# Hybrid encoder block on one core: output tiles between the attention's last blocks, first loads of the second layer on GpSimd's queue, results added one a step

## The chip, the cores and the metric

The kernel runs on one NeuronCore of a Trainium2 chip. Five engines work side by side: TensorE (PE, with its weight loads shown as PEld), VectorE (DVE), ScalarE (ACT), GpSimd (POOL) and SyncE (SP), which issues DMAs. Each engine takes its own instructions in order and waits on semaphores for the others. The metric is the device time of one execution in microseconds, as the median of several runs; lower is better.

## The reference

One block of a streaming encoder on 1024 tokens (and 16 meta tokens in front, dropped at the end) of width 1024, all in float32:

```
u = rmsnorm(h, norm_mix);  z = u @ w_in            # pool input, q, k, v, r, low rank gate, ga, gb
y_a = pooled means (windows 2, 4, 8, 16) mixed by group, scaled, @ w_pool_out
y_b = (rmsnorm(chunked gated linear attention(q, k, v)) * silu(r)) @ w_gla_out
h = h + (sigmoid(ga) * y_a + sigmoid(gb) * y_b) @ w_out
u = rmsnorm(h, norm_ffn)
h = h + square(relu(u @ w_ff1)) @ w_ff2            # 1024 -> 4096 -> 1024
out = rmsnorm(h, norm_final)
```

## The kernel before

**Products.** Every float32 operand of a product is split in two: ACT makes a rounded high part (`act.activation(hi, a, ACT.Copy)`), DVE or GpSimd subtracts it to get the low part, and `mm3` (L250) issues three matmuls of 128x512 for each pair of operand tiles. So each loaded weight costs a DMA, an ACT operation and a DVE operation before PE can use it.

**Order.** PE's instructions run in the order in which the program writes them (L1463). The order of the other engines, SP's queue of DMA issues included, is made by a planner from its own model of the times, with the program's order as priority; on the chip each of these engines then works its list in order and waits at whatever is not ready.

**From the attention to the first layer.** Tokens are two halves of 512. The list `one` holds the steps. `gla` (L1099) runs the attention and fills PE's gaps with other blocks, last the four `yb_block(j, 0)` of the first half. What follows is the second half: `yb_block(j, 1)` (L859), j = 0 to 3, each 24 matmuls on a quarter of w_gla_out, merged by DVE with the gates (`t<-gb_dram`) and the pooled part (`o<-ma_dram`), L880 to L885, into `MH`, `ML`. `out_tile(t, 0)` (L1182) multiplies 128 tokens of the merged result with the first 512 columns of w_out, 24 matmuls, and adds x, which lies in `acc` (L1195). Tiles 0 to 3 read the first half only, 4 to 7 the second. Its weights `wo` come in four quarters, `load_wo(0, k)` (L1157): quarter k holds contraction tiles 2k and 2k + 1, in the order in which the tile uses them. `x_again` (L1153) loads x into `acc`, eight tiles.

**Raw buffers.** Both kinds of weights land in raw buffers that `Raw.load` (L93) takes in rotation; there are two, and a third is lent by `merge_open` (L1150). The ring `W1` (L57) holds the split form of two blocks: `top_up` (L66) loads the block after the next one as soon as a block has issued its last matmul ("free", L879), and it issues load and split in one go, so a raw buffer stays taken until the ring's slot is free and both split operations are done. In the program, the load of block j + 2 stands at the end of block j.

**Second layer.** The first layer writes seven combinations of its squared results to DRAM (`keep`, L1304), from SP's queue. The second layer, `ff2` (L1401), is a Strassen-like scheme of seven products, m = 0 to 6, of 16 steps each. A step multiplies one loaded tile `a` (`ff2_load`, L1346, into one of four half buffers) with one weight tile (`ff2_weight`, L1351; the four quarters of w_ff2 stay in SBUF) or a sum of two (`bt`, L1375), for four token tiles t: 12 matmuls. Operands are split two steps ahead into seven slots. The accumulators are four PSUM banks of eight, in turn. After a product's last step the program adds all its results to `c` (`leave`, L1411): one or two DVE operations a token tile, for m = 4 also the finished rows of tokens 512 to 1023 (`finish_row`, L1379), for m = 5 the last normalization's upper half (L1435 to L1439), for m = 6 the other rows, which end the program.

Of the kernel before, what the change touches and what calls it, by code (L numbers as in the profile page):

```python
# [10 lines left out]
ACT = mybir.ActivationFunctionType  # L11
ALU = mybir.AluOpType
AX = mybir.AxisListType

P = 128
# [4 lines left out]
HALF = 512  # L20
# [83 lines left out]
def kernel(  # L104
# [3 lines left out]
    nc = tc.nc  # L108
    x = x[0]
# [50 lines left out]
    gB = left.push("gB", [P, D], F32)  # L160
# [27 lines left out]
    def f32(ap):  # L188
        return ap.bitcast(F32)
# [4 lines left out]
    def bcast(v):  # L194
        return v[None, :].broadcast_to([P, D])
# [248 lines left out]
    def halves():  # L444
        return [slice(h * HALF, (h + 1) * HALF) for h in range(2)]
# [213 lines left out]
    one = []  # L659
# [122 lines left out]
    def rows4(w, j):  # L782
        return w[:, j * 256 : (j + 1) * 256].rearrange("(k p) c -> p k c", p=P)
# [75 lines left out]
    def yb_block(j, h):  # L859
        def fn(wb):  # L860
            hi, lo = (t.rearrange("p (k c) -> p k c", k=4) for t in wb)
            assert h or ("o", 0) in done
            yg = S["yg"][h]
            for e in range(2):
                d, w = 2 * j + e, slice(e * P, (e + 1) * P)
                yb_load(d, h)
                yb_load(d + 1, h)
                if S["dt1"] > 3:
                    yb_load(d + 2, h)
                gl, ml = staged[d, h]  # L870
                b = bank("mm")
                for k in range(4):
                    mm3(
                        b, 1, lambda i: (hi[:, k, w], lo[:, k, w]),
                        lambda i: (yg[:, 0, k], yg[:, 1, k]), first=k == 0, last=k == 3,
                    )
                    yield 3 * 512 / 2400
                if e:
                    yield "free"  # L879
                dve.tensor_tensor(gl, b, gl, ALU.mult)  # L880
                dve.tensor_tensor(gl, gl, ml, ALU.add)
                th = MH[h][:, d]
                tl = ML[h][:, d]
                act.activation(th, gl, ACT.Copy)
                pool.tensor_tensor(tl, gl, f32(th), ALU.subtract)  # L885

        return fn
# [250 lines left out]
    def merge_open():  # L1138
        W1.eng = dve
        banks(keep=2, ms=3)  # L1140
        left.pop_to(base)
        right.pop_to(1)
        S["wo"] = [left.push("wo0", [P, 2, KT, HALF], F32R)]
        S["left_acc"] = left.mark()
        S["acc"] = left.push("acc", [P, 8, D], F32)
        buffer("u2", 2, D)
        S["left2"] = left.mark()
        buffer("t1", 4)
        buffer("o", 4)
        raw.lend(left.push("raw3", [P, D], F32))  # L1150
        nc.sync.dma_start(gB, bcast(norm_ffn))

    def x_again():  # L1153
        for t in range(8):
            nc.sync.dma_start(S["acc"][:, t], x[t * P : (t + 1) * P, :])

    def load_wo(ch, kk):  # L1157
        def fn():
            wo = S["wo"][ch][:, :, 2 * kk : 2 * kk + 2]
            c = slice(ch * HALF, (ch + 1) * HALF)  # L1160
            r = raw.load(w_out[kk * 256 : (kk + 1) * 256, c].rearrange("(k p) c -> p k c", p=P), D)
            r = r.rearrange("p (k c) -> p k c", k=2)
            act.activation(wo[:, 0], r, ACT.Copy)
            dve.tensor_tensor(wo[:, 1], r, f32(wo[:, 0]), ALU.subtract)

        return fn
# [15 lines left out]
    def out_tile(t, ch):  # L1182
        def fn():
            half, at = t // 4, (t % 4) * P
            wo = S["wo"][ch]
            b, n = bank("mm"), ORDER.index(t)
            for j in range(2):
                if ch and j and n > 1:
                    turn_tile(ORDER[n - 2])
                mm3(  # L1190
                    b, KT // 2, lambda i: (MH[half][:, 4 * j + i, at : at + P], ML[half][:, 4 * j + i, at : at + P]),
                    lambda i: (wo[:, 0, 4 * j + i], wo[:, 1, 4 * j + i]), first=j == 0, last=j == 1,
                )
# [38 lines left out]
            dve.tensor_tensor(fl, a, f32(fh), ALU.subtract)  # L1232

    yb = lambda j: step(one, yb_block(j, 1), W1, [rows4(w_gla_out, j)])
    yb(0)
    for k in range(4):
        step(one, load_wo(0, k))
    yb(1)
    yb(2)
    step(one, x_again)  # L1240
    step(one, out_tile(0, 0))
    yb(3)
    step(one, out_tile(1, 0))
    step(one, wo1_open)
    for t in range(2, 8):
        step(one, out_tile(t, 0))
        if t < 6:
            step(one, load_wo(1, t - 2))

# [52 lines left out]
    hf_of = {m: hf_dram[n] for n, (m, _, _) in enumerate(FF2)}  # L1302
# [42 lines left out]

    def ff2_load(m, i):  # L1346
        at = S["a2"][(m * NPAIR + i) % len(S["a2"])]
        nc.sync.dma_start(at, hf_of[FF2[m][0]][i])
        return at

    def ff2_weight(q, i):  # L1351
        j, k = int(q[0]) - 1, int(q[1]) - 1
        f = 2 * i + j
        nc.sync.dma_start(S["w2"][q][:, i], w_ff2[f * P : (f + 1) * P, k * HALF : (k + 1) * HALF])

    def ff2_raw():
        for m in range(7):
# [21 lines left out]
    def finish_row(t, tail):  # L1379

        a, (h0, h1) = S["c"][:, t], halves()
        junk = S["w2"]["12"].rearrange("p i c -> p (i c)")[:, (t % 4) * D : (t % 4 + 1) * D]
        if not tail:
            ss = ln_stat[t % 4]
            act.activation(junk, a, ACT.Square, accum_out=ss)
            rs = inv_sqrt(ss, 1, 1.0 / D)
            dve.scalar_tensor_tensor(junk, a, rs, gB, ALU.mult, ALU.mult)
# [12 lines left out]

    def ff2():  # L1401
        nc.sync.dma_start(gB, bcast(norm_final))
        h1 = halves()[1]
        b, late = None, []

        def product(t, i, av, bv):
            (ah, al), (bh, bl) = av, bv
            c = slice(t * P, (t + 1) * P)
            mm3(b[t], 1, lambda _: (ah[:, c], al[:, c]), lambda _: (bh, bl), first=i == 0, last=i == NPAIR - 1)

        def leave(m, t):  # L1411
            for r, k, sign in FF2[m][2]:
                a = S["c"][:, 4 * r + t, k * HALF : (k + 1) * HALF]
                if sign > 0:
                    dve.tensor_tensor(a, b[t], a, ALU.add)
                else:
                    dve.tensor_tensor(a, a, b[t], ALU.subtract)

        for m, i, av, bv in ahead(ff2_operands(), 2):
            if i == 0:  # L1420
                b = [bank("o") for _ in range(4)]
            if m == 6 and i >= NPAIR - 3:
                late.append((i, av, bv))
            else:
                for t in range(4):
                    product(t, i, av, bv)
            if i < NPAIR - 1:
                continue
            for t in range(4):
                for x in late:  # L1430
                    product(t, *x)
                leave(m, t)
                if m == 4:
                    finish_row(4 + t, False)
                elif m == 5:  # L1435
                    a = S["c"][:, t, h1]
                    junk = S["w2"]["12"][:, 8 + t]
                    act.activation(junk, a, ACT.Square, accum_out=tails[t][1])
                    dve.tensor_tensor(a, a, gB[:, h1], ALU.mult)  # L1439
                elif m == 6:  # L1440
                    finish_row(t, True)

    def ff_layers():

# [59 lines left out]
```

## Time and profile before

| | |
|---|---|
| median of 3 runs | 1255.62 us (1255.46 to 1256.19) |
| the profiled execution | 1256.39 us |
| its span, first to last instruction | 1254.6 us |
| granted clock of TensorE, mean | 0.998 |
| busy: PE, DVE, ACT, POOL | 97%, 68%, 50%, 5% |
| DMA | 175.40 MB, 140 GB/s over the span |

Busy times are sums over stages with different limits, so the profile is read stage by stage: which engine waits, for how long, and what ended the wait. A row of the timeline gives start, duration, engine, source line and operation, and in brackets the idle time ahead of it with what ended it. SPq rows are DMA issues.

### The profile page before, as it was taken

The numbers are of one execution on the slowest core, as the hardware profiler recorded it, in microseconds if no ns is written. First come the engines' busy times: TensorE is split into PE (matmuls) and PEld (weight loads), VectorE is DVE, ScalarE is ACT, GpSimd is POOL, SyncE is SP. The second block draws the span as 40 slices with busy tenths as digits, with TensorE's granted clock in tenths as the row PEclk, the third lists the DMA queues.
The fourth block names the chain that finished last, engine by engine and source line by source line (L and its number), as shares of the span: only waits on it lengthen the run. The fifth ranks groups of instructions, "written<-read, shape, count | busy, mean of one in ns | idle before, by whom it ended". The sixth has DMA issues, their size and how long they took to land.

```text
span 1254.6 us, 18159 instructions
## 1 busy us (share of the span) xinstructions
PE 1212.4 (97%) x6799; PEld 1001.8 (80%) x6799; DVE 850.0 (68%) x1404; ACT 625.4 (50%) x1101; POOL 57.5 (5%) x37
## 2 busy tenths in 40 slices
PE   3999999999999999999999999999999999999997
PEld 2888888988897877788878888888878788888776
DVE  6776667564355766842897776766764877887686
ACT  7557747431345565422664554554553444445544
POOL 0000000001000114500000000000000000000000
PEclk9999999999999999999999999999999999999999
DMA  8023334417211236850244544544569863333532
GB/s 265 1 67 109 110 92 127 142 54 249 85 36 35 86 109 194 302 202 37 81 130 150 167 150 143 168 145 149 164 221 380 271 231 108 96 98 88 173 89 88
DMA packets 143863, 175.40 MB, mean 140 GB/s; under 512 B 11008, under 2 KB 83472, under 8 KB 143776
## 3 DMA queue, kind: packets, MB, share of 16 engines
q1 hardware_dynamic: 143776, 174.25, 43.4%
q8 instruction: 53, 0.87, 0.3%
q14 instruction: 34, 0.28, 0.1%
HBM read 120.74 MB, written 53.48 MB: 139 GB/s over the span
## 4 chain that ended last, share of the span: by engine, by line
PE 90%; DVE 4%; ACT 2%; DMA 2%; issue 2%; SPq 0%; DVEq 0%; ACTq 0%
PE b_mm L254 9%; PE b_mm L256 9%; PE b_mm L255 9%; PE b_o L255 8%; PE b_o L256 8%; PE b_o L254 8%; PE b_y L254 5%; PE b_y L255 5%; PE b_y L256 5%; PE b_z L254 3%; PE b_z L255 3%; PE b_z L256 3%; PE b_sc L255 3%; PE b_sc L254 3%; PE b_sc L256 3%
## 5 line engine op out<-in xcount | busy, mean ns | idle before, releaser
L254 PE MATMUL b_mm<-th,w1h 128*128 128x512 f32 (+1 forms) x240 | 86.1, 359 | 0.0
L255 PE MATMUL b_mm<-tl,w1h 128*128 128x512 f32 (+1 forms) x240 | 83.9, 349 | 0.0
L256 PE MATMUL b_mm<-th,w1l 128*128 128x512 f32 (+1 forms) x240 | 83.7, 349 | 0.0
L272 ACT ACTIVATE w1h<-raw 128x512 fp32r<-128x512 f32 x96 | 59.6, 623 | 43.3 <-PE b_sc L255 14.1
L254 PE MATMUL b_sc<-th,w1h 128*128 128x512 f32 x192 | 76.8, 400 | 2.0 <-ACT u2p L364 2.0
L254 PE MATMUL b_o<-w1h 128*128 128x512 f32 x192 | 75.0, 390 | 2.8 <-DVE h L1312 1.8
L255 PE MATMUL b_sc<-tl,w1h 128*128 128x512 f32 x192 | 76.3, 398 | 0.3 <-DVE tl L199 0.3
L255 PE MATMUL b_o<-w1l,w1h 128*128 128x512 f32 x192 | 75.0, 390 | 1.4 <-DVE w1l L273 1.4
L256 PE MATMUL b_sc<-th,w1l 128*128 128x512 f32 x192 | 75.8, 395 | 0.0
L256 PE MATMUL b_o<-w1h,w1l 128*128 128x512 f32 x192 | 74.8, 390 | 0.1
L273 DVE TENSOR_TENSOR w1l<-raw,w1h 128x512 fp32r<-128x512 f32 x96 | 65.6, 684 | 10.9 <-ACT w1h L272 10.9
L272 ACT ACTIVATE w1h<-fs 128x512 fp32r<-128x512 f32 x72 | 45.4, 631 | 49.9 <-PE b_y L255 34.4
L254 PE MATMUL b_z<-th,w1h 128*128 128x512 f32 x160 | 62.5, 391 | 0.4 <-DVE c L618 0.4
L255 PE MATMUL b_z<-tl,w1h 128*128 128x512 f32 x160 | 62.4, 390 | 0.4 <-DVE tl L1224 0.4
L256 PE MATMUL b_z<-th,w1l 128*128 128x512 f32 x160 | 62.3, 389 | 0.0
L273 DVE TENSOR_TENSOR w1l<-fs,w1h 128x512 fp32r<-128x512 f32 x72 | 49.3, 685 | 17.9 <-ACT w1h L272 17.9
L1375 DVE TENSOR_TENSOR bt<-w,w 128x512 f32<-128x512 f32 x80 | 54.6, 683 | 1.7 <-DMA w<-in_w_ff_dram 1.7
L272 ACT ACTIVATE w1h<-bt 128x512 fp32r<-128x512 f32 x44 | 27.6, 629 | 54.6 <-issue 31.4
L254 PEld LDWEIGHTS b_mm<-th,w1h 128*128 128x128 f32 x240 | 45.0, 188 | 8.8 <-issue 2.3
L254 PE MATMUL b_mm<-wo,th 128*128 128x512 f32 x128 | 50.4, 394 | 0.0
L256 PEld LDWEIGHTS b_mm<-th,w1l 128*128 128x128 f32 x240 | 45.1, 188 | 6.0
L256 PE MATMUL b_o<-fxh,fxl 128*128 128x512 f32 x128 | 49.9, 390 | 0.0
(334 smaller groups left out, 3386.7 us busy)
## 6 DMA issues: line engine op xcount, KB each, us to landing
hf_dram<-h SPq DMA_DIRECT2D x112, 256.0 KB, 2.1
raw<-hf_dram SPq DMA_DIRECT2D x112, 256.0 KB, 2.7
w<-in_w_ff_dram SPq DMA_DIRECT2D x64, 256.0 KB, 4.9
raw<-in_w_in_dram SPq DMA_DIRECT2D x24, 512.0 KB, 4.7
raw<-in_w_ff_dram SPq DMA_DIRECT2D x16, 512.0 KB, 4.2
rawx<-in_w_ff_dram SPq DMA_DIRECT2D x16, 512.0 KB, 4.1
xs<-in_x_dram SPq DMA_DIRECT2D x8, 512.0 KB, 5.6
rawx<-in_w_in_dram SPq DMA_DIRECT2D x8, 512.0 KB, 4.5
```

What stands on the lines that cost most here:

```text
L254: pe.matmul(ps, ah, bh, start=first and i == 0, stop=False, skip_group_check=more)
L255: pe.matmul(ps, ah, bl, start=False, stop=False, skip_group_check=more)
L256: pe.matmul(ps, al, bh, start=False, stop=last and i == n - 1, skip_group_check=more)
L272: act.activation(hi, a, ACT.Copy)
L273: dve.tensor_tensor(lo, a, f32(hi), ALU.subtract)
L1375: dve.tensor_tensor(bt, w, S["w2"][q[3:]][:, i], ALU.add if q[2] == "+" else ALU.subtract)
```

## The change

Three parts. The order of steps at the end of the attention: out tiles 0 and 1 of the first half stand after the second and third of the last blocks instead of after the third and fourth, three of the four quarters of w_out are loaded after the second block, and each out tile loads its own x tile. The load of norm_ffn's weights into `gB` moves from `merge_open` to the out tile 4. In the second layer, the loads of steps 0 to 3 of the first product, hf tiles and weight quarter "11", eight DMAs, go through GpSimd's queue. The results of products 0 to 5 are kept in a list `owed`, and each later step issues one entry; those of the last product are issued at once as before.

```
-        nc.sync.dma_start(gB, bcast(norm_ffn))
-    def x_again():
-        for t in range(8):
-            nc.sync.dma_start(S["acc"][:, t], x[t * P : (t + 1) * P, :])
+    def x_again(t):
+        nc.sync.dma_start(S["acc"][:, t], x[t * P : (t + 1) * P, :])
...
+    def out_(t):
+        def fn():
+            x_again(t)
+            if t == 4:
+                nc.sync.dma_start(gB, bcast(norm_ffn))
+            out_tile(t, 0)()
+        step(one, fn)
     yb(0)
-    for k in range(4):
+    step(one, load_wo(0, 0))
+    yb(1)
+    for k in range(1, 4):
         step(one, load_wo(0, k))
-    yb(1)
+    out_(0)
     yb(2)
-    step(one, x_again)
-    step(one, out_tile(0, 0))
+    out_(1)
     yb(3)
-    step(one, out_tile(1, 0))
     step(one, wo1_open)
     for t in range(2, 8):
-        step(one, out_tile(t, 0))
+        out_(t)
         if t < 6:
             step(one, load_wo(1, t - 2))
...
     def ff2_load(m, i):
-        nc.sync.dma_start(at, hf_of[FF2[m][0]][i])
+        queue(m, i).dma_start(at, hf_of[FF2[m][0]][i])
+    def queue(m, i):
+        return pool if m == 0 and i < 4 else nc.sync
     def ff2_weight(q, i):
-        nc.sync.dma_start(S["w2"][q][:, i], ...)
+        (queue(0, i) if q == "11" else nc.sync).dma_start(S["w2"][q][:, i], ...)
...
+        def add(b, t, r, k, sign):
+            a = S["c"][:, 4 * r + t, k * HALF : (k + 1) * HALF]
+            if sign > 0:
+                dve.tensor_tensor(a, b, a, ALU.add)
+            else:
+                dve.tensor_tensor(a, a, b, ALU.subtract)
+        def top(t):
+            a = S["c"][:, t, h1]
+            act.activation(S["w2"]["12"][:, 8 + t], a, ACT.Square, accum_out=tails[t][1])
+            dve.tensor_tensor(a, a, gB[:, h1], ALU.mult)
         def leave(m, t):
+            for at in FF2[m][2]:
+                owed.append(lambda b=b[t], at=at: add(b, t, *at))
+            if m == 4:
+                owed.append(lambda: finish_row(4 + t, False))
+            elif m == 5:
+                owed.append(lambda: top(t))
+            elif m == 6:
+                owed.append(lambda: finish_row(t, True))
         for m, i, av, bv in ahead(ff2_operands(), 2):
...
+            if owed:
+                owed.pop(0)()
             if i < NPAIR - 1:
                 continue
             for t in range(4):
                 for x in late:
                     product(t, *x)
                 leave(m, t)
+                while m == 6 and owed:
+                    owed.pop(0)()
```

More of the change, by code (lines that the diff above doesn't have):

```diff
@@ L1353, in ff2_weight @@
         f = 2 * i + j
-        nc.sync.dma_start(S["w2"][q][:, i], w_ff2[f * P : (f + 1) * P, k * HALF : (k + 1) * HALF])
+        (queue(0, i) if q == "11" else nc.sync).dma_start(S["w2"][q][:, i], w_ff2[f * P : (f + 1) * P, k * HALF : (k + 1) * HALF])
     def ff2_raw():
@@ L1403, in ff2 @@
         h1 = halves()[1]
-        b, late = None, []
+        b, late, owed = None, [], []
         def product(t, i, av, bv):
@@ L1409, in product @@
             mm3(b[t], 1, lambda _: (ah[:, c], al[:, c]), lambda _: (bh, bl), first=i == 0, last=i == NPAIR - 1)
-        def leave(m, t):
[L1412 to L1417, printed above, removed]
+        def add(b, t, r, k, sign):
[8 more added lines that the diff above has]
+            dve.tensor_tensor(a, a, gB[:, h1], ALU.mult)
+        def leave(m, t):
+            for at in FF2[m][2]:
[6 more added lines that the diff above has]
+                owed.append(lambda: finish_row(t, True))
         for m, i, av, bv in ahead(ff2_operands(), 2):
@@ L1432, in ff2 @@
                 leave(m, t)
[L1433 to L1441, printed above, removed]
+                while m == 6 and owed:
+                    owed.pop(0)()
     def ff_layers():
```

## The prediction

> **What bounds the kernel now.** I read the page first, then TensorE's (PE's) waits, then the stretch of each large wait engine by engine.
>
> ```profile
> PE 1212.4 (97%) x6799; PEld 1001.8 (80%) x6799; DVE 850.0 (68%) x1404; ACT 625.4 (50%) x1101; POOL 57.5 (5%) x37
> ...
> PE b_mm L254 <- ACT w1h L75: 1.4, 1, 1.4
> PE b_o L254 <- DVE h L1312: 1.8, 1, 1.8
> PE b_o L255 <- DVE w1l L273: 1.4, 1, 1.4
> PE b_mm L256 <- DVE w1l L76: 1.1, 1, 1.1
> PE b_o L254 <- ACT w1h L272: 1.0, 1, 1.0
> PE b_o L255 <- DVE small L215: 0.7, 1, 0.7
> ```
>
> PE is busy 97% of the span, and its instruction order is fixed. The change takes no product away, so it can gain only these six waits, 7.4 us in all, and what the clock loses after them; it can lose by making new ones. The two b_mm waits belong to the third block of the second half's `yb` (call the four blocks Y0 to Y3), the four b_o waits to the second layer.
>
> ```profile
> 517.42 0.39 PE L256 MATMUL b_mm<-yg,w1l 128*128 128x512 f32 x1
> 519.21 0.50 PE L254 MATMUL b_mm<-yg,w1h 128*128 128x512 f32 x1 [1.40 <-ACT w1h L75]
> 519.54 0.40 PE L255 MATMUL b_mm<-yg,w1h 128*128 128x512 f32 x1
> 521.06 0.50 PE L256 MATMUL b_mm<-yg,w1l 128*128 128x512 f32 x1 [1.12 <-DVE w1l L76]
> ...
> 521.60:525.00 3.40, 3.40 (x10) 2.63 (x9) 2.27 (x3) 0.90 (x2) 1.51 (x1) 0.51 0.76 208
> 525.10:528.20 3.10, 3.10 (x15) 2.55 (x14) 1.58 (x3) 2.11 (x3) 0.82 (x1) 1.00 1.06 382
> 528.20:533.60 5.40, 5.40 (x25) 4.46 (x25) 3.52 (x5) 1.29 (x2) 2.01 (x2) 1.00 1.04 406
> ```
>
> The first four rows are PE's timeline, the others windows (the last three columns are granted clock, DMA share and GB/s). Y1 ends at 517.8, Y2 waits for its weights until 521.06, and then the clock is 0.51 for 3.4 us, which costs 1.7 us more. The DMA engines are full at 382 to 406 GB/s.
>
> **Change, part 1: out tiles between the last blocks.** Matmul count and the bytes moved stay. What moves is the order: Y0, first quarter of w_out (Q0), Y1, Q1 to Q3, out tile O0, Y2, O1, Y3, where it was Y0, Q0 to Q3, Y1, Y2, O0, Y3, O1. O0 contracts over all of w_out, so it needs all four quarters. They and Y's weights pass through three raw buffers in rotation. Before: Y2's weights in the first, Q0 second, Q1 third, Q2 first, Q3 second, Y3's weights third. After: Y2's, Q0, Y3's, then Q1 in the first, Q2 in the second, Q3 in the third. Q1 now has to wait until Y2's weights are split, Q3 until Y3's are.
>
> ```profile
> 503.90 0.38 SPq L99 DMA_DIRECT2D raw<-in_w_out_dram  x1
> ...
> 512.24 0.38 SPq L99 DMA_DIRECT2D raw<-in_w_gla_out_dram  x1
> 512.66 1.14 SPq L99 DMA_DIRECT2D raw<-in_w_out_dram  x2
> ...
> 521.03 0.38 SPq L99 DMA_DIRECT2D raw<-in_w_out_dram  x1
> ...
> 522.17 0.38 SPq L99 DMA_DIRECT2D raw<-in_w_gla_out_dram  x1
> ...
> SPq L99 <- DVE w1l L76: 2.7, 2, 1.9
> ...
> 507.65 1.06 ACT L1163 ACTIVATE wo<-raw 128x1024 fp32r<-128x1024 f32 x1 [1.00 <-DMA raw<-in_w_out_dram]
> ...
> 518.11 1.04 ACT L75 ACTIVATE w1h<-raw 128x1024 fp32r<-128x1024 f32 x1
> ...
> 525.54 1.06 ACT L1163 ACTIVATE wo<-raw 128x1024 fp32r<-128x1024 f32 x1 [2.13 <-DMA raw<-in_w_out_dram]
> ...
> 519.19 1.82 DVE L76 TENSOR_TENSOR w1l<-raw,w1h 128x1024 fp32r<-128x1024 f32 x1 [0.65 <-ACT w1h L75]
> 520.93 1.21 DVE L1164 TENSOR_TENSOR wo<-raw,wo 128x1024 fp32r<-128x1024 f32 x1
> ...
> 528.00 0.69 DVE L880 TENSOR_TENSOR t<-b_mm,t 128x512 f32<-128x512 f32 x1 [1.37 <-PE b_mm L256]
> ```
>
> These are SyncE's (SP's) DMA issues, its waits, and the ACT and DVE timelines. The load at 512.24 is Y2's. It can start only when DVE has split Y1's weights, and that does not change. Its split ends at 521.01 (519.19 + 1.82), and the load at 521.03, held by that split, was Q2. In the changed kernel the load in this place is Q1. It lands at 525.54 (that ACT row begins there), ACT takes 1.06, DVE 1.21: high part at 526.6, low part at 527.8.
>
> PE meanwhile ends Y1 at 517.8 and does the six products of O0 that need Q0 only, to 519.2. Then it stands until 526.6 for one product and until 527.8 for the rest: some 8.4 us instead of the 2.5 us now. 17 products remain, at 0.225 us (5.4 us for O0's 24 in the last window) 3.8 us, to 531.6; the half clock adds 1.7, to 533.3. The same number of products (Y0, Y1 and 24 more) is now done at 528.0, when DVE reads Y2's last bank. **Part 1 costs 5.3 us.** No later wait before 622 us gives it back: Y2's and Y3's weights are by then split, but PE has the same work left.
>
> Bounds: the fastest w_out landing shown is 3.75 us (503.90 to 507.65). With it for Y2's load too, and a split of 1.21 instead of 1.82, Y2's split ends at 518.3, Q1's at 524.3, and O0 at 529.8: still 1.8 us lost. Upwards: Q3 waits in the third buffer for Y3's weights, which are behind Y2's on ACT and DVE (522.2 at the earliest, the time of the last issue above). x rows for the tile can also pass ahead of it.
>
> ```profile
> acc<-in_x_dram SPq DMA_DIRECT2D x8, 512.0 KB, 8.1
> ```
>
> If Q3 takes those 8.1 us it is split at 532.6, and with five products and the cold clock O0 ends near 535.5: 7.5 us lost. I take the middle chain, because its rows are this very load in this very queue.
>
> The `x_again` loads go from one batch of eight to one a tile, and norm_ffn's to tile 4: the same bytes, needed only by O0's DVE addition and the second output half, and hidden behind 5.4 us of PE work per tile. Without that cover each x load costs 1.3 us (512 KB at 406 GB/s).
>
> On the clock, the Trainium skill (TensorE: Matmul & The Clock Gate, "What's actually happening") has a free-running window of about 3.4 us that must be busy before full rate returns. A restart in the middle of a window could then run cold for two of them, an estimate of 1.7 us more; the one cold stretch here was 3.4 us long, so the sum stays with that.
>
> **Part 2: eight first loads of the second layer on GpSimd's queue.** Four hf loads and four w_ff2 tiles leave SP's queue, in which they stand behind the stores of the first layer's last results.
>
> ```profile
> SPq L1306 <- ACT h L1315: 9.1, 3, 6.9
> ...
> 937.28 0.47 PE L254 MATMUL b_o<-w1h 128*128 128x512 f32 x1 [1.76 <-DVE h L1312]
> ...
> 976.65 0.50 PE L254 MATMUL b_o<-w1h 128*128 128x512 f32 x1 [1.01 <-ACT w1h L272]
> ...
> 910.00:940.00 30.00, 28.23 (x125) 23.08 (x124) 20.68 (x34) 16.60 (x28) 0.00 (x0) 1.00 0.65 217
> 940.00:973.00 33.00, 33.00 (x148) 27.31 (x147) 15.08 (x25) 13.34 (x22) 0.00 (x0) 1.00 1.02 377
> ```
>
> The first stall, at 937.28, is not a load: PE waits for PSUM until DVE has added the first layer's last result. Earlier splits can at best take one of them (0.6 us of DVE) from in front of that addition; its other predecessors are first-layer work. The second, 1.0 us, is loads at the end of a stretch in which the DMA engines are full (1.02). Bytes moved into the stretch before, which is at 0.65, make it shorter: 1 MB at 377 GB/s is 2.8 us, enough to end that stall. I take 1.0 us gained, from the two: between nothing and 2.1 (the whole second stall and 1.1 of the first).
> GpSimd issues no DMA in this trace. Its nearest row is its own 128x512 subtraction.
>
> ```profile
> 541.04 1.29 POOL L885 TENSOR_TENSOR tl<-t,th 128x512 fp32r<-128x512 f32 x1 [1.43 <-ACT th L884]
> ```
>
> It is GpSimd's last work, so nothing is queued behind the eight issues but themselves. At 1.29 us each they take 10.3 us and would be done some 5 us before 937 even if none started before 921, when the first layer's operands leave that memory. If DVE slows beside them as its split above did (1.82 for 1.21), eight times 0.6 us fall into a stretch where DVE has 9 us free; at worst, 1 us of it shows. Bound: +1.0.
>
> On this part the Trainium skill (DMA: Bandwidth & Descriptors, "Issuing engines are not separate DMA queues") speaks against a gain: all queues share the same DMA engines, and another issuer saves only issue time. By it part 2 is worth nothing, and the sum below would be 1258.5.
>
> **Part 3: results added one a step.** The last two b_o waits are bursts at the change of product: four finished rows at 1162, twelve DVE operations at 1207, queued ahead of the splits that PE needs.
>
> ```profile
> 1162.42 0.39 PE L254 MATMUL b_o<-fxh,w1h 128*128 128x512 f32 x1
> 1163.52 0.50 PE L255 MATMUL b_o<-fxl,w1h 128*128 128x512 f32 x1 [0.71 <-DVE small L215]
> ...
> 1207.00 0.39 PE L254 MATMUL b_o<-w1h 128*128 128x512 f32 x1
> 1208.76 0.50 PE L255 MATMUL b_o<-w1l,w1h 128*128 128x512 f32 x1 [1.38 <-DVE w1l L273]
> ...
> L1387 DVE SCALAR_TENSOR_TENSOR w<-c,small,gB 128x1024 f32<-128x1024 f32 x4 | 5.1, 1283 | 0.0
> L1375 DVE TENSOR_TENSOR bt<-w,w 128x512 f32<-128x512 f32 x70 | 47.8, 682 | 0.0
> ```
>
> The gaps are 1.10 and 1.76 us where 0.225 is the pace: 2.4 us lost. Spread, a step of 12 products (2.7 us) carries three operations of 0.68 us and one addition, 2.7 us of DVE at most; the steps with a finished row carry two splits and about 1.28 + 0.67 (four small ones), 3.3 us, but every other one only 2.0. Operands are made two steps ahead, so that evens out. Banks: a product's four are free for the product after the next, 16 steps on, and the last addition is at step 12. **Gain 2.4 us**; bounds 0 (the wait only moves to later steps) and 2.4. The end of the program keeps its order.
>
> **Sum.** +5.3 - 1.0 - 2.4 = +1.9. The profiled execution took 1256.39 us (span 1254.6 and 1.8 around it), so 1258.3; the runs' median lies 0.8 below that execution: **1257.5 us**. About 0.2% (2.5 us: 1253.1 to 1258.1) is what a measurement can tell from no change, so I forecast no change that shows, on the slow side.
>
> **Rivals.**
> Slower, third buffer: Q3 decides instead of Q1, behind Y3's weights and x rows, as bounded: +7.5 - 1.0 - 2.4, 1259.7. It decides once Q3 lands after some 529. For it: DMA at 1.0 share there. Against: Q3 has 2.7 us of O0's products as slack.
> Slower, the later parts pay nothing: DVE's order is a planner's, which may keep the bursts, and part 2 frees nothing: +5.3, 1260.9. For it: DVE already interleaves additions with splits.
> Faster, the tile covers the load: all quarters are split by the time O0 asks, O0's 5.4 us bridge Y2's wait, and 2.5 + 1.7 go: -4.2 - 1.0 - 2.4, 1248.0. For it: two w_out loads did go out at 512.66, before Y2 began. Against: the rotation above ties Q1 to Y2's split.
> Short chain: part 1 at its bound of 1.8, the others at theirs, -2.1 and -2.4: 1252.9.
>
> **Chances.** Forecast 0.50 (0.08 of it above 1258.1); third buffer 0.17; nothing paid 0.11; short chain 0.07 (0.05 of it within 0.2%); cover 0.15. Faster 0.17, same 0.47, slower 0.36. The range leaves out the cover case and 0.05 at the top: 1251.5 to 1261.5. The forecast's own is 1255.5 to 1259.
>
> **What would show it.** Part 1: a PE wait of 7 us or more in O0 for ACT or DVE `wo`, no wait in Y2, a stretch of half clock behind it. Part 2: hf and w loads on GpSimd before 930, no wait near 975 plus the shift. Part 3: no b_o waits for L215 or L273 late. I am wrong if O0 runs without a wait, or if the rows of the second layer show new ones.

## The result, and the profile after

| | kernel before | changed kernel | ratio, 95% interval |
|---|---|---|---|
| median of the first six executions each | 1255.78 us | 1262.65 us (1261.85 to 1265.00) | 1.0058 [1.0045, 1.0071] |
| a second series, four executions against 25 | 1256.11 us | 1262.8 us (1261.27 to 1263.37) | 1.0054 [1.0040, 1.0067] |
| profiled execution | 1256.39 us, span 1254.6 | 1265.00 us, span 1263.2 | |

The change makes the kernel slower by about 0.6%. The forecast was 1257.5 us, with a range to 1261.5; the result lies above both. The profiled execution is the longest of its six, some 2.3 us above their median, which matters for part 2 below. Three executions that took 2473 us (the changed kernel, the profiled one of the second series), 3133 us (the kernel before) and 6915 us (part 3 alone) were disturbed from end to end and are left out of every figure, so the second series has no trace.

PE's waits of the changed kernel, from the view of waits (engine, line, what was waited for: us in all, times, longest):

```profile
PE b_mm L254 <- ACT wo L1161: 10.5, 1, 10.5
...
PE b_o L254 <- DVE h L1321: 1.9, 1, 1.9
...
PE b_z L254 <- DVE h L1321: 1.2, 1, 1.2
```

The two b_mm waits of before (1.4 and 1.1 us, in Y2) are gone, and so are the three late b_o waits for L272, L273 and L215. In their place stand a wait of 10.5 us in O0 and a new one of 1.2 us in the second layer. The lines have moved: L1161 and L1162 are the splits of w_out (L1163 and L1164 before), L1321 is the second layer's addition (L1312 before).

The 10.5 us, on the timelines of SP, ACT, DVE and PE of the changed kernel (start, duration, engine, line, and in brackets the idle time before and what ended it):

```profile
512.95 0.38 SPq L99 DMA_DIRECT2D raw<-in_w_gla_out_dram  x1
517.75 0.32 SPq L856 DMA_DIRECT2D t<-gb_dram  x1
...
519.45 0.32 SPq L856 DMA_DIRECT2D t<-gb_dram  x1
519.82 0.42 SPq L857 DMA_DIRECT2D o<-ma_dram  x1
520.30 0.42 SPq L99 DMA_DIRECT2D raw<-in_w_gla_out_dram  x1
520.77 1.37 SPq L99 DMA_DIRECT2D raw<-in_w_out_dram  x2
522.18 0.47 SPq L1153 DMA_DIRECT2D acc<-in_x_dram  x1
...
528.04 1.06 ACT L1161 ACTIVATE wo<-raw 128x1024 fp32r<-128x1024 f32 x1 [2.18 <-DMA raw<-in_w_out_dram]
529.35 1.06 ACT L1161 ACTIVATE wo<-raw 128x1024 fp32r<-128x1024 f32 x1 [0.26 <-DMA raw<-in_w_out_dram]
...
530.46 0.79 PE L254 MATMUL b_mm<-wo,th 128*128 128x512 f32 x1 [10.51 <-ACT wo L1161]
...
538.60 0.69 DVE L1193 TENSOR_TENSOR acc<-b_mm,acc 128x512 f32<-128x512 f32 x1 [4.40 <-PE b_mm L256]
...
SPq L856 <- POOL tl L885: 6.8, 3, 4.3
```

Y2's weights leave at 512.95, as before. Then SP issues nothing for 4.4 us: next in its order stand two pairs of gating loads (`t<-gb_dram`, `o<-ma_dram`, for column tiles 4 and 5), which wait for their buffers (the last row is from SP's waits between 500 and 535 us: the longest, 4.3 us, is for GpSimd's subtraction, which reads `t`). Behind them Y3's weights leave at 520.30, Q2 at 520.77 and Q1, as soon as Y2's weights are split, at 521.8. Three loads of 512 KB and an x row block are in the DMA engines together. Q2 lands first (its split begins at 528.04), Q1 at 529.3 (529.35). PE, in order, needs Q1 first and stands until 530.46.

Where each part's loss or gain lies is read by matching matmuls: all these kernels issue the same 6799 in the same stretches, so the start of the same-numbered one in two traces tells how far one kernel is behind. Before O0 (before's row at 517.42, shown with the prediction) the changed kernel is 0.78 us behind, all of it from the first 15 us; at 636 us it is 10.58 behind:

```profile
518.20 0.39 PE L256 MATMUL b_mm<-yg,w1l 128*128 128x512 f32 x1
...
646.61 0.40 PE L256 MATMUL b_sc<-th,w1l 128*128 128x512 f32 x1
```
```profile
636.03 0.39 PE L256 MATMUL b_sc<-th,w1l 128*128 128x512 f32 x1
```

The first two rows are of the changed kernel, the third is the same matmul before. Each ratio is to the executions of the kernel before in the same series (medians 1255.8 to 1256.4). The last three columns are worked out in this way from one profiled execution each, with the points at which the kernel before stands at 517.4 and 636.4, at 929.7 and 990.4, and at 1153.6 and 1224.3 us (positive is lost against the kernel before):

| kernel | median us | ratio, 95% interval | part 1's stretch | part 2's | part 3's |
|---|---|---|---|---|---|
| whole change | 1262.65 | 1.0058 [1.0045, 1.0071] | +9.80 | +1.26 | -2.75 |
| part 1 alone | 1264.69 | 1.0064 [1.0050, 1.0077] | +8.34 | -0.01 | -0.04 |
| part 1, gating loads later | 1262.48 | 1.0044 [1.0029, 1.0059] | +4.27 | +0.01 | -0.06 |
| part 1, quarters first | 1259.28 | 1.0020 [1.0010, 1.0029] | +1.15 | +0.02 | +0.01 |
| the same, four raw buffers, gating loads later | 1255.25 | 0.9995 [0.9986, 1.0005] | -1.17 | +0.03 | +0.01 |
| part 2 alone | 1254.99 | 0.9988 [0.9979, 0.9997] | -0.20 | -0.62 | -0.02 |
| part 2, hf loads only | 1256.71 | 1.0006 [0.9997, 1.0015] | -0.15 | +0.02 | +0.01 |
| part 3 alone | 1253.49 | 0.9977 [0.9966, 0.9989] | +0.29 | -0.14 | -2.75 |
| parts 2 and 3 | 1252.82 | 0.9974 [0.9964, 0.9984] | +0.03 | -0.47 | -2.74 |
| all parts, quarters first, four buffers, gating later | 1253.15 | 0.9977 [0.9968, 0.9987] | -1.19 | +1.01 | -2.75 |
| all parts but w tiles, gating loads, then quarters | 1250.94 | 0.9962 [0.9949, 0.9974] | -2.20 | +0.05 | -2.75 |
| whole change, gating loads, then quarters | 1252.22 | 0.9971 [0.9958, 0.9983] | -2.55 | +0.06 | -2.75 |

Stretches that an edit does not touch agree with before within 0.3 us, which is how far such a difference can be trusted. By medians, the parts alone (+8.8, -0.9, -2.4) make +5.4; the whole change measured +6.9, and the intervals are wide enough for the 1.5 between.

### The profile page after: what moved, and what is told of

Its sections match the earlier page's. It is cut to its first block, busy times and chain, and to the rows that moved or that the text cites. A ratio compares the mean times of both kernels' runs of the same rounds, so it can differ in the third digit from the quotient of the medians.

```text
span 1263.2 us, 18214 instructions
## 1 busy us (share of the span) xinstructions
PE 1214.0 (96%) x6799; PEld 1004.5 (80%) x6799; DVE 852.2 (67%) x1404; ACT 624.6 (49%) x1101; POOL 61.6 (5%) x45
## 4 chain that ended last, share of the span: by engine, by line
PE 89%; DVE 4%; DMA 3%; ACT 2%; issue 2%; SPq 0%; POOL 0%; DVEq 0%; ACTq 0%; POOLq 0%
PE b_mm L254 9%; PE b_mm L255 9%; PE b_mm L256 9%; PE b_o L254 8%; PE b_o L255 8%; PE b_o L256 8%; PE b_y L254 5%; PE b_y L256 5%; PE b_y L255 5%; PE b_z L254 3%; PE b_z L255 3%; PE b_sc L255 3%; PE b_sc L254 3%; PE b_z L256 3%; PE b_sc L256 3%
## 5 line engine op out<-in xcount | busy, mean ns | idle before, releaser
L272 ACT ACTIVATE w1h<-raw 128x512 fp32r<-128x512 f32 x96 | 59.4, 621 | 32.4 <-PE b_sc L255 14.2
L273 DVE TENSOR_TENSOR w1l<-raw,w1h 128x512 fp32r<-128x512 f32 x96 | 65.7, 685 | 12.4 <-ACT w1h L272 12.3
L272 ACT ACTIVATE w1h<-fs 128x512 fp32r<-128x512 f32 x72 | 45.4, 631 | 50.0 <-PE b_y L255 34.3
L254 PE MATMUL b_mm<-wo,th 128*128 128x512 f32 x128 | 51.7, 404 | 10.5 <-ACT wo L1161 10.5
L272 ACT ACTIVATE w1h<-bt 128x512 fp32r<-128x512 f32 x44 | 27.8, 632 | 67.1 <-issue 61.2
L273 DVE TENSOR_TENSOR w1l<-fs,w1h 128x512 fp32r<-128x512 f32 x72 | 49.4, 686 | 17.2 <-ACT w1h L272 17.2
L255 PE MATMUL b_mm<-wo,th 128*128 128x512 f32 x128 | 51.2, 400 | 0.5 <-DVE wo L1162 0.5
L256 PE MATMUL b_mm<-wo,tl 128*128 128x512 f32 x128 | 50.9, 397 | 0.0
```

What stands on the lines that cost most here:

```text
L254: pe.matmul(ps, ah, bh, start=first and i == 0, stop=False, skip_group_check=more)
L255: pe.matmul(ps, ah, bl, start=False, stop=False, skip_group_check=more)
L256: pe.matmul(ps, al, bh, start=False, stop=last and i == n - 1, skip_group_check=more)
L273: dve.tensor_tensor(lo, a, f32(hi), ALU.subtract)
```

## The experiments

### Part 1 alone

The second layer stays as before; of the diff only the order list, `x_again(t)` and `out_` are taken.

```diff
 yb(0)
-for k in range(4):
-    step(one, load_wo(0, k))
+step(one, load_wo(0, 0))
 yb(1)
+for k in range(1, 4):
+    step(one, load_wo(0, k))
+out_(0)
 yb(2)
-step(one, x_again)
-step(one, out_tile(0, 0))
+out_(1)
```

> Part 1 alone: the first half's output tiles between the blocks and the weight quarters behind the second block; the second layer is that of the kernel before. Theory (late Q1): the loads of two gating tiles stand ahead of Y3's weights and of Q1 to Q3 in SyncE's queue, Q1 is issued near 521.8, lands near 529, TensorE stands 10 to 11 us in the first output tile and comes back to two windows of half clock, about 3 us of work lost. Together +8 to +10, so 1263.5 to 1265.5, slower than the whole change. Rival (the forecast's own chain, with the rest of the loss in parts 2 and 3): +5.3, 1261.1. Rival (the tile covers the load): 1251 to 1253.

Measured: 1264.69 us against 1255.92. The theory's size holds; PE's row is

```profile
529.43 0.79 PE L254 MATMUL b_mm<-wo,th 128*128 128x512 f32 x1 [9.87 <-ACT wo L1161]
```

and no more than 0.1 us is lost or given back later (8.74 us behind at 636, 8.64 at 1224). So part 1 alone costs more than the whole change shows, and the forecast's +5.3 was too small.

### Part 1 with the gating loads later

Of the second block's loads, those for column tiles 4 and 5 are left to the third block. Buffers and everything else are as in part 1.

```diff
             yb_load(d, h)
-            yb_load(d + 1, h)
-            if S["dt1"] > 3:
+            if not (h and d == 3):
+                yb_load(d + 1, h)
+            if S["dt1"] > 3 and not (h and j == 1):
                 yb_load(d + 2, h)
```

> Part 1 alone, with the gating loads that the second block makes ahead for the third (two pairs, for column tiles 4 and 5) left to the third block itself, so that they no longer stand in SyncE's queue ahead of Y3's weights and of Q1 and Q2. The rotation of the three raw buffers is as in part 1. Theory (late Q1): Y3's weights and Q2 are issued near 513 to 514 instead of 520.3 and 520.8, they no longer share the DMA engines with Q1, and Q1 lands near 525.5 to 527 instead of 529: the wait in the first output tile is 7 to 8.5 us instead of 10.5, and the time is 2 to 4 us below part 1 alone. A cost against it: the third block may now wait for its gating tiles. Rival (rotation alone decides, the queue's order does not matter): Q1 lands at 529 as in part 1, and the time is that of part 1 alone within 1 us.

Measured: 1262.48 us, 2.2 less than part 1 alone in the same series, with a wait of 6.6 us in O0. SP's, ACT's and PE's timelines of this kernel:

```profile
513.40 0.94 SPq L99 DMA_DIRECT2D raw<-in_w_gla_out_dram  x2
514.38 0.57 SPq L99 DMA_DIRECT2D raw<-in_w_out_dram  x1
...
522.22 1.51 SPq L99 DMA_DIRECT2D raw<-in_w_out_dram  x2
...
525.89 1.06 ACT L1162 ACTIVATE wo<-raw 128x1024 fp32r<-128x1024 f32 x1 [1.30 <-DMA raw<-in_w_out_dram]
...
527.00 0.79 PE L254 MATMUL b_mm<-wo,th 128*128 128x512 f32 x1 [6.60 <-ACT wo L1162]
```

Y2's and Y3's weights now leave together at 513.4, Q2 at 514.4, and when Q1 leaves at 522.2 these have landed and only Q3 is behind it: it lands 3.7 us later, at 525.9, where in the whole change it took 7.6 (521.8 to 529.3). While Q1 is under way the DMA engines are busy for 0.63 of the time here, at 215 GB/s (522.2 to 525.9), against 0.97 and 334 GB/s in the whole change (521.8 to 529.3). The rotation of the buffers is the same in both, so what took Q1 from 525.9 to 529.3 is the loads beside it: Y3's weights, Q2 and the x rows, which here leave at 516.48. They are beside it because they stood behind the gating loads. That is shown for the three together; how much each of them costs is not. What is left, 4.3 us in this stretch, I put down to the rotation (Q1 behind Y2's split) with its clock; the next runs bear on that.

### Quarters first

All four quarters are loaded ahead of Y0, so that none passes through a buffer that holds Y2's or Y3's weights.

```diff
+for k in range(4):
+    step(one, load_wo(0, k))
 yb(0)
-step(one, load_wo(0, 0))
 yb(1)
-for k in range(1, 4):
-    step(one, load_wo(0, k))
 out_(0)
```

> Part 1 alone, with all four quarters of w_out loaded ahead of block Y0 instead of behind Y0 and Y1. Then Q1 to Q3 do not go through a buffer that holds Y2's or Y3's weights, and no gating load stands ahead of Q1 and Q2; Y2's and Y3's weights go behind the quarters. Theory (part 1 loses only by the late quarters): the wait of 10 us in O0 shrinks to 3 us or less, Y2's own waits of 2.5 us go since O0's 24 products stand in front of it, time between 1251.5 and 1256. Rival (the DMA engines are what is short, whatever the order): some load, then Y2's or Y3's, is as late as Q1 was, and the time stays above 1260.

Measured: 1259.28 us, between the two expectations. The large wait is gone; three small ones are left:

```profile
518.25 0.50 PE L254 MATMUL b_mm<-wo,th 128*128 128x512 f32 x1 [0.63 <-ACT wo L1161]
519.89 0.50 PE L255 MATMUL b_mm<-wo,th 128*128 128x512 f32 x1 [1.14 <-DVE wo L1162]
527.54 0.50 PE L255 MATMUL b_mm<-wo,th 128*128 128x512 f32 x1 [1.56 <-DVE wo L1162]
```

Three buffers for six loads still hold two quarters back: in SP's timeline one leaves at 512.06, when Y1's weights are split, and the last at 519.87, when that quarter's own split frees its buffer; the last row above is the last quarter's. This profiled execution took 1256.89 us, while the ten executions lie between 1255.93 and 1261.07 at one granted clock (0.996 to 0.997). What the longer ones lose, no trace shows; it stays open.

### Quarters first, four raw buffers, gating loads later

Both causes of the late quarters are taken away at once: the order of the last run and the later gating loads of the one before it stay, and a fourth buffer is added. No run has the fourth buffer alone.

```diff
-        raw.lend(left.push("raw3", [P, D], F32))
+        raw.lend(left.push("raw3", [P, D], F32), left.push("raw4", [P, D], F32))
```

> Part 1 alone with the quarters ahead of Y0, and besides with a fourth raw buffer and without the gating loads that the second block makes ahead. Theory: every load of this stretch has its buffer and its place early enough; no wait in O0 or in Y2, no half clock there, 2.5 + 1.7 us less than the kernel before: 1251.5 to 1252.5. If the wait in the run with three buffers was gone already, the two are equal within 1 us.

Measured: 1255.25 us, no difference from before that can be told, and 2.8 us above the top of the expected range. No wait for `wo` is left, but two others came:

```profile
513.07 0.37 SPq L99 DMA_DIRECT2D raw<-in_w_out_dram  x1
513.49 0.46 SPq L857 DMA_DIRECT2D o<-ma_dram  x1
...
520.55 0.47 PE L254 MATMUL b_mm<-wo,th 128*128 128x512 f32 x1 [1.97 <-DVE t L881]
527.73 0.50 PE L256 MATMUL b_mm<-yg,w1l 128*128 128x512 f32 x1 [1.00 <-DVE w1l L76]
```

One quarter goes through the buffer of Y1's weights and leaves at 513.07, when these are split. In SP's order the gating loads for Y1's own tiles stand behind it, so DVE takes Y1's PSUM bank late, and PE waits 1.97 us for that bank. It is the first fault with the places exchanged: a load that waits for a buffer holds back the loads behind it that would have needed none.

### All parts on that layout

The same edits on the whole change.

> All three parts, with the quarters ahead of Y0, four raw buffers and the gating loads left to the third block. Theory, parts add up (-4.2 for part 1 so laid out, -1.0 and -2.1 as parts 2 and 3 measured alone): 1248.7. Rival (part 2 costs where the waits near 937 and 943 fall badly): 1250 to 1251.

Measured: 1253.15 us. Parts 1 and 3 do what they did alone (-1.19 and -2.75), part 2's stretch loses 1.01. So the rival is nearer, though not by its numbers; more under part 2.

### Gating loads, then quarters

The gating tiles 0 to 3 are issued first, and the rotation begins with the two lent buffers, so that only Q3 passes through a buffer whose block is unsplit. The w_ff2 tiles stay on SP's queue.

```diff
-        raw.lend(left.push("raw3", [P, D], F32))
+        raw.slots = [left.push("raw3", [P, D], F32), left.push("raw4", [P, D], F32)] + raw.own
...
+step(one, lambda: [yb_load(d, 1) for d in range(4)])
+for k in range(4):
+    step(one, load_wo(0, k))
 yb(0)
-step(one, load_wo(0, 0))
 yb(1)
-for k in range(1, 4):
-    step(one, load_wo(0, k))
...
-    (queue(0, i) if q == "11" else nc.sync).dma_start(S["w2"][q][:, i], ...)
+    nc.sync.dma_start(S["w2"][q][:, i], ...)
```

> All three parts, with the loads of the first four gating tiles ahead of the quarters, all quarters ahead of Y0, four raw buffers (the two lent ones first in the rotation, so that Q0 to Q2 need no buffer of a block that is still unsplit), and of part 2 only the hf loads on GpSimd's queue. Theory: the run with quarters first kept two waits in this stretch, 2.0 us for DVE t (its gating tile had been issued behind a quarter that waited for Y1's split, at 513.1) and 1.0 us for Y2's low part; with the gating tiles ahead the first goes, so part 1 gains 3 to 4.2 us, part 3 2.1, part 2 nothing or 1: 1248.5 to 1251. Rival (the bytes of the stretch are what is short: two megabytes of gating tiles ahead of the quarters make the quarters late): a wait for wo of 2 us or more in O0, and 1253 or more.

Measured: 1250.94 us, 0.9962 [0.9949, 0.9974]: faster than both kernels, and the lowest median of this study, inside the expected range though part 1 gives less than the 3 to 4.2 us expected of it. SP's timeline and PE's waits:

```profile
510.87 1.72 SPq L99 DMA_DIRECT2D raw<-in_w_out_dram  x3
512.90 0.37 SPq L99 DMA_DIRECT2D raw<-in_w_gla_out_dram  x1
...
519.13 0.50 PE L254 MATMUL b_mm<-wo,th 128*128 128x512 f32 x1 [0.49 <-ACT wo L1161]
520.47 0.50 PE L255 MATMUL b_mm<-wo,th 128*128 128x512 f32 x1 [0.84 <-DVE wo L1162]
```

All quarters and Y2's weights have left by 513.3, some eight microseconds before Q1 does in the changed kernel. Two short waits are left, no stretch of half clock follows, and part 1's order gains 2.20 us where it cost 9.80. So the order of the tiles is sound; what made it slow is the order of the loads under it and the buffers that they share.

### Part 2 alone

```diff
-        nc.sync.dma_start(at, hf_of[FF2[m][0]][i])
+        queue(m, i).dma_start(at, hf_of[FF2[m][0]][i])
...
-        nc.sync.dma_start(S["w2"][q][:, i], ...)
+        (queue(0, i) if q == "11" else nc.sync).dma_start(S["w2"][q][:, i], ...)
```

> Part 2 alone: the four hf loads and the four w_ff2 tiles on GpSimd's queue. Theory (ScalarE held at a weight): the first of the four w tiles lands near 940, ScalarE waits for it some 3 us in order, with the first layer's last split behind it; a new wait of TensorE for DVE h of 1 us or more appears some 5 us behind the first b_o wait, with half clock behind it, and the wait near 975 goes. Net +0.5 to +1.6: 1256.3 to 1257.4. Rival (the forecast's step): the wait near 975 goes and none is new, -1.0: 1254.8. Rival (queues share the DMA engines, issue alone changes): 0, 1255.8, and the wait near 975 stays.

Measured: 1254.99 us against 1255.92, the rival's number (the forecast's own), but not by its mechanism: there is a new wait, and it is the theory's, without the half clock (the clock is 1.00 from 930 to 945). In the trace the stretch loses 1.35 us up to 941 and gains 1.97 from the wait near 976 on. The loss, on ACT's, DVE's and PE's timelines of this kernel:

```profile
929.17 0.63 ACT L272 ACTIVATE fxh<-w 128x512 fp32r<-128x512 f32 x1 [2.75 <-DMA w<-in_w_ff_dram]
929.71 0.61 ACT L272 ACTIVATE w1h<-raw 128x512 fp32r<-128x512 f32 x1
...
930.35 0.69 DVE L273 TENSOR_TENSOR w1l<-raw,w1h 128x512 fp32r<-128x512 f32 x1 [2.01 <-ACT w1h L272]
...
932.16 0.68 DVE L1312 TENSOR_TENSOR h<-b_z,u3p 128x512 f32<-128x512 f32 x1
...
932.99 0.47 PE L254 MATMUL b_z<-th,w1h 128*128 128x512 f32 x1 [0.93 <-DVE h L1312]
```

and the same operations in the kernel before:

```profile
927.57 0.62 ACT L272 ACTIVATE w1h<-raw 128x512 fp32r<-128x512 f32 x1
929.09 0.63 ACT L272 ACTIVATE fxh<-w 128x512 fp32r<-128x512 f32 x1 [0.90 <-DMA w<-in_w_ff_dram]
...
928.99 0.68 DVE L273 TENSOR_TENSOR w1l<-raw,w1h 128x512 fp32r<-128x512 f32 x1
...
931.32 0.69 DVE L1312 TENSOR_TENSOR h<-b_z,u3p 128x512 f32<-128x512 f32 x1
```

The first w tile is split at the same time in both (929.17 and 929.09; the theory's 940 was read from the changed kernel, where that row stands at 940.36). But ACT's written order has changed: the tile's split now stands ahead of two others, and these wait behind it for 2.75 us. One of them (`w1h`) feeds DVE's split at 930.35, behind which stand, in DVE's order, the additions that empty PE's banks; so PE waits for a bank.

### Part 2, hf loads only

The four w_ff2 tiles go back to SP's queue.

> Of part 2 only the four hf loads on GpSimd's queue, the four w_ff2 tiles stay on SyncE's. Theory (in part 2 alone the w tiles made the new wait of TensorE for DVE h near 932, ScalarE standing in order at a weight tile): no wait for DVE h before the one near 937; the wait near 976 stays or is shorter; between -1.0 and 0: 1255.0 to 1256.0. Rival (the hf loads make it, through DVE's earlier splits): the wait near 932 is there as in part 2 alone.

Measured: 1256.71 us, 1.0006 [0.9997, 1.0015]. No wait for DVE h before the one near 937, and the wait near 976 is as it was: the stretch differs by 0.02 us. The hf loads on GpSimd's queue change nothing that can be told; gain and loss of part 2 come with the w tiles. No run moves the w tiles without the hf loads.

### Part 3 alone

```diff
-                if m == 4:
-                    finish_row(4 + t, False)
+            for at in FF2[m][2]:
+                owed.append(lambda b=b[t], at=at: add(b, t, *at))
+            if m == 4:
+                owed.append(lambda: finish_row(4 + t, False))
...
+            if owed:
+                owed.pop(0)()
```

> Part 3 alone: the second layer's results are added one a step. Theory: the two bursts late in the second layer go, PE's waits for the small DVE operations near 1163 and for the DVE split near 1208 with them, -2.4 to -2.8: 1253.0 to 1253.4. Rival (the waits only move to later steps): 0, 1255.8.

Measured: 1253.49 us, 2.4 less than before and 0.1 above the expected range (the later expectations take it as -2.1, from a median with the 6915 us in it); the two late waits are gone from the list of waits and none is new. The trace's 2.75 us comes back within 0.01 in every kernel that has part 3.

### Parts 2 and 3

> Parts 2 and 3 without part 1: what the change is worth without its first part. If they add up: -1.0 - 2.1, 1252.9. Rival (each hides in the other, since both move the second layer's DVE work): 1253.9, as part 3 alone.

Measured: 1252.82 us. They add up within the noise (-3.2 together, -0.9 and -2.4 alone).

### The changed kernel again

No edit.

> The changed kernel once more, for a second profiled execution: the first one was the slowest of its six (1265.0 against a median of 1262.7). Its rows showed two losses behind the O0 wait: a second wait of 1.2 us near 943 with a stretch of half clock near 950 (about 2.5 us together). Theory (they hang on where the waits fall against the clock's windows): this execution lies near the median and has no half clock near 950, the wait in O0 stays at 10 to 11 us. Rival (both belong to the kernel): the half clock near 950 is there again.

The times were 1261.27 to 1263.37 us, at mean granted clocks of 0.992 to 0.995. The question of the half clock near 950 can only be answered from times: of the ten executions of this kernel in both series the five at 0.991 or 0.992 took 1262.75 to 1265.00 us, the five at 0.993 to 0.995 took 1261.27 to 1263.37. That fits stretches of half clock that come in some executions and not in others, which favours the theory; without a second trace it is not shown.

### The whole change with its loads mended

The layout of the 1250.94 kernel with all of part 2.

> The whole change (all of part 2 too), with only the loads around the first output tiles laid out anew: gating tiles first, quarters ahead of Y0, four raw buffers with the lent ones first. Against the run with hf loads alone on GpSimd it adds the four w_ff2 tiles. Theory (the w tiles bring the gain near 976 and 988, some 1.3 us, and make the wait near 932, 1.1 us; half clock may follow where that wait and the next fall into one window): -0.5 to +1 against 1250.9, so 1250.4 to 1252. Rival (part 2 is worth its 1.0 here as alone): 1249.9.

Measured: 1252.22 us, just above the theory's range and well above the rival. The two medians are 1.3 us apart, but they are of two series whose kernel before differs by 0.4; each against its own, the w tiles on GpSimd's queue cost 0.9 us (-4.2 against -5.1), with overlapping intervals, so no difference is shown. The profiled executions differ little (1251.21 and 1250.94); the longer ones of this kernel, 1254.57 and 1254.64, are those at a mean clock of 0.996 and 0.995, the shorter have 0.997 to 0.999.

## Why the prediction was wrong

**The sum.** In the profiled execution the three stretches come to +8.3 where +1.9 was forecast. Of the 6.4 us between, 4.5 are part 1's and 2.3 part 2's, less 0.35 that part 3 gained on its forecast. By medians the miss is 5.0.

**Part 1: direction and chain right, size wrong (+5.3 forecast, +8.3 and +9.8 measured).** The step that failed is "It lands at 525.54". Everything up to it held: the load in the place of the old Q2 is Q1, and it was issued at 521.8 less the 0.78 of the start, 521.0, as forecast. I took its duration from the old row, 4.5 us. That row belongs to a load with few others beside it: the DMA engines moved 208 GB/s then (521.6 to 525.0, shown with the prediction), because the other quarters had gone at 512.66. I moved Q1 in SP's order but not the loads around it: the prediction lists what the step issues, and forgot that Y1, now ahead of Q1 to Q3, brings its gating loads for two tiles with it, that these wait for buffers until 519.5, and that a queue issued in order holds Y3's weights and Q2 behind them until they meet Q1. The measured landing was 529.3. With the gating loads out of the way it was 525.9, and O0 ended at 533.60, or 532.4 less that kernel's 1.24 of the start, where the chain had said 533.3: the forecast's chain was that of a kernel with another queue.

The second step is "the half clock adds 1.7". In the sum of the whole change's 9.8 us, the later restart (530.46 less 0.78, against 526.6) is 3.1 and the run-out from there to the end of O0 is 1.4 more than forecast. The windows of the changed kernel (us, PE, PE's weight loads, DVE, ACT, GpSimd; granted clock, DMA share, GB/s):

```profile
530.40:536.80 6.40, 5.87 (x13) 4.30 (x14) 2.45 (x2) 1.07 (x2) 0.00 (x0) 0.50 1.00 382
536.80:537.80 1.00, 1.00 (x4) 0.76 (x4) 0.00 (x0) 0.00 (x0) 0.00 (x0) 0.65 1.06 412
```

The clock stays at half until about 537.5, 7.0 us after PE took up its work. The prediction put the Trainium skill's free-running window (TensorE: Matmul & The Clock Gate, "What's actually happening") beside the sum, with 1.7 us more by it, and kept to the one cold stretch of before. The trace agrees with the page here, and the sum should have carried it.

**The bounds.** The upper bound of 7.5 was built from Q3 and x rows. Q3 landed at 531.9, late as feared, but was not what PE waited for: Q1 was later still for its place. The rival "slower, third buffer" therefore did not happen. "The later parts pay nothing" came nearest in time, 1260.9, for a wrong reason, since part 3 paid in full. The rival "the tile covers the load" is what the mended layout comes to, without all of its 4.2 us.

**Part 2: -1.0 forecast; -0.9 measured alone, +1.3 in the whole change's trace.** The gain is larger than I took: 1.97 us, all of it at and behind the wait near 976; the bound of 2.1 that I halved had counted 1.0 there and 1.1 at the first stall, which got longer. That more is moved in the stretch before fits the trace of part 2 alone (376 GB/s from 930 to 940, 319 in the kernel before), but no run tests it by itself. The loss has another cause and size than "at worst, 1 us of it shows" for DVE beside GpSimd: it is the order on ACT, which I did not look at, because I took the planner's order as given when a load moves to another queue. It is 1.4 to 2.0 us in the five profiled kernels that have it. So it is luck that part 2 alone came out near the forecast's -1.0: that is the difference of a gain and a loss, both of another size than forecast. And in two of those five, the whole change and the first full layout, a stretch of half clock follows:

```profile
949.00:953.40 4.40, 4.29 (x13) 3.44 (x14) 2.97 (x5) 1.67 (x3) 0.00 (x0) 0.67 0.99 355
```

which costs 1.6 us more and turns the part's sign there. That explains the difference between the whole change's profiled execution and part 2 alone; how often it comes, the traces at hand do not tell. The Trainium skill's rule (DMA: Bandwidth & Descriptors, "Issuing engines are not separate DMA queues") that another issuer saves only issue time holds for the hf loads, at 0.02 us in their stretch. It does not cover the w tiles, where what changed was the time at which they leave and the order of the engine that splits them.

**Part 3: -2.4 forecast, -2.75 in the traces, -2.4 in medians.** Mechanism and size held, the waits did not move to later steps, and the end of the program is as it was.

**What would show it.** A wait of 7 us or more in O0 for `wo`, none in Y2, half clock behind it, none near 975, none for L215 or L273: all seen. "No later wait gives it back" held too (10.6 us behind at 528, 10.58 at 636). "hf and w loads on GpSimd before 930" held for the hf loads and, less the 10.2 us by which the kernel was late there, for the w tiles (932.70). The rows of the second layer did show a new wait, named there as what would make me wrong.

## What to carry to other kernels

When a step moves past others in an in-order queue, write out that queue again, with every load that now stands ahead of the one on the path and what each waits for; a duration taken from an old row holds only while the same loads are in flight beside it. Loads that wait for nothing go ahead of loads that wait for a buffer, and the order of compute was worth 2.2 to 2.6 us here once that was so, against 8 to 10 lost when it was not. When a load changes queues, look at the order in which the consuming engine takes it, not only at when it lands.

## What the runs showed of the hardware

How long the clock stayed low after a long wait differed: 7.0 us in the changed kernel (the windows above, after a wait of 10.5), 5.5 in part 1 alone (after 9.9), 3.7 with the gating loads later (after 6.6). The windows of these last two, in that order:

```profile
529.40:534.40 5.00, 4.50 (x10) 3.22 (x11) 2.45 (x2) 1.06 (x1) 0.00 (x0) 0.50 0.97 356
534.40:535.40 1.00, 1.00 (x5) 0.82 (x4) 0.00 (x0) 0.00 (x0) 0.00 (x0) 0.75 1.04 424
```
```profile
527.00:530.00 3.00, 2.53 (x5) 1.74 (x6) 1.28 (x2) 1.06 (x1) 0.00 (x0) 0.50 0.98 342
530.00:531.00 1.00, 1.00 (x4) 0.75 (x4) 1.00 (x1) 0.00 (x0) 0.00 (x0) 0.66 1.06 408
```

The clock also fell where no single wait was long. In the first full layout PE waited 0.96 and, some five microseconds later, 1.94 us, and then ran at half; in the mended change the waits were 1.59 and 1.94 us at the same places, and the clock stayed full:

```profile
931.72 0.47 PE L254 MATMUL b_z<-th,w1h 128*128 128x512 f32 x1 [0.96 <-DVE h L1321]
936.64 0.47 PE L254 MATMUL b_o<-w1h 128*128 128x512 f32 x1 [1.94 <-DVE h L1321]
...
938.00:942.00 4.00, 4.00 (x13) 3.15 (x13) 1.69 (x4) 1.08 (x2) 0.00 (x0) 0.63 1.03 384
```
```profile
931.73 0.47 PE L254 MATMUL b_z<-th,w1h 128*128 128x512 f32 x1 [1.59 <-DVE h L1321]
936.65 0.47 PE L254 MATMUL b_o<-w1h 128*128 128x512 f32 x1 [1.94 <-DVE h L1321]
...
936.00:940.00 4.00, 3.35 (x15) 2.79 (x16) 3.51 (x6) 1.81 (x4) 0.00 (x0) 1.00 0.99 346
940.00:945.00 5.00, 5.00 (x24) 4.14 (x23) 3.21 (x6) 1.87 (x5) 0.00 (x0) 1.00 0.95 349
```

The changed kernel (1.2 and 1.9 us) lost time to half clock there, parts 2 and 3 (1.1 and 1.9) did not. So in these traces two waits of one to two microseconds cost another 1.6, or nothing, and their sum does not tell which.

GpSimd's loads go through a queue of another kind, as the profile's page of the changed kernel lists it (`software_dynamic`); each took GpSimd 0.5 us to issue, against 0.3 to 0.5 on SP, so the prediction's 1.29 us, taken from its subtraction, was more than double (the second row, from GpSimd's timeline, has the four w tiles together):

```profile
q0 software_dynamic: 640, 2.10, 0.6%
...
932.70 2.13 POOL L1367 DMA_DIRECT2D w<-in_w_ff_dram  x4 [11.49 <-PE b_sc L256]
```
